# The row of 1/rms made by two transfers through HBM

## Chip, cores and metric

One core of one Trainium2 chip runs the whole program. The metric is the device time of the program in microseconds (us). TensorE (PE) multiplies matrices and reads its weights through a load path of its own (PEld), VectorE (DVE), ScalarE (ACT) and GpSimd (POOL) work element by element, SyncE (SP) issues transfers. Every engine runs its own list of instructions in order, and an instruction that waits holds up all that stand behind it on that engine.

## The reference

Two layers of a block over 512 tokens with 1024 channels. Each layer normalizes the tokens by their root mean square, projects them into five kinds of columns (pooled inputs, queries, keys, values, two gates), mixes, and closes with a gated feed-forward part:

```
def rmsnorm(x, g):
    xf = x.astype(jnp.float32)
    y = xf * lax.rsqrt(jnp.mean(xf * xf, axis=-1, keepdims=True) + NORM_EPS)
    return (y * g.astype(jnp.float32)).astype(x.dtype)

xn = rmsnorm(x, norm1_g[i])
proj = xn @ w_in[i]
u_pool, q, k, v, g_a, g_b = jnp.split(proj, splits, axis=-1)
...
merged = jax.nn.sigmoid(g_a) * pool_out + jax.nn.sigmoid(g_b) * attn_out
x = x + merged @ w_out[i]
```

The scale 1/rms is one number for each token.

## The kernel before

Every matrix product is made of three: operands are split into a rounded half and the rest (`whi`, `wlo` of the weights, `xh`, `xl` of the activations, `qh`, `ql` of queries and keys), and high by high, high by low and low by high are added up in PSUM. L289 to L291 and L308 to L310 are these three matmuls; a weight block of 512 KB is loaded into `raw` (L225, one of 7 buffers), cast by ACT into `whi`, and DVE makes `wlo` of it (both L213).

The activations go into the products without the 1/rms of their tokens; it is applied to what comes out. `token_stats` (L439, L440) sums squares on PE and lets POOL make `stats[:, 1, :]`, a tile in which partition p, column t holds 1/rms of token 128 t + p. Where a product has tokens on the partitions (queries, keys, values, the second gate), ACT and DVE scale by such a column. The pooled inputs and the first gate are made with tokens along the free axis (`windowed`, L714, and `merged`, L748); these need 1/rms as a row of 512 that stands on all 128 partitions. That row is `rms_rows[layer]`, the second half of a tile named `hg`, made once a layer by `spread_rms` (L500 to L506): four transposes on PE (L315) of the columns, each broadcast over 128, into a PSUM bank, and a copy by ACT (L506).

The order of the work is written with a counter of PE columns, `clock`: each matmul or transpose adds what it takes (a transpose 256). `later(delay, what)` asks for a piece of work when the counter has gone on by `delay`; before each triple of matmuls, `run_due` runs what is due. `spread_rms` is asked for 81600 columns behind a layer's start. Between the program's text and each engine's list stands the framework's scheduler, which settles where an instruction stands when the program is built; so a transfer can stand in SP's list well ahead of where the counter would put it.

SP's list holds the loads of weights and the turning of blocks of queries, keys, probabilities and outputs: DVE turns them in squares of 32, then a transfer takes them to HBM (`away`, L324) and four bring them back (`near`, L328). A load waits until its `raw` buffer is free, that is, until `wlo` of an earlier block is made. In layer 0 the first queries and keys are turned on PE (L315, `ident,qn`) and not through HBM.

The functions that the change touches, and what calls them:

Of the kernel before, what the change touches and what calls it, by code (L numbers as in the profile page):

```python
# [10 lines left out]
F32 = mybir.dt.float32  # L11
# [7 lines left out]
P = 128  # L19
# [3 lines left out]
NT = S // P  # L23
# [31 lines left out]

QK_AWAY, SCORE_AWAY, PROB_AWAY, AV_AWAY, MERGE_AWAY = 28000, 26000, 32000, 18000, 24000
NORMED, ROTATED, JOINED, GATED, SUMMED, GATE = 7200, 2400, 2400, 4800, 9600, 2400
HIDDEN_DELAYS = (26000, 28000), (8000, 14000)


# [64 lines left out]
def trunk_kernel(  # L125
# [10 lines left out]
    nc = tc.nc  # L136
# [3 lines left out]
    hbm = ctx.enter_context(tc.tile_pool(name="hbm", bufs=1, space=bass.MemoryType.DRAM))  # L140
# [29 lines left out]
    rotary, rms_rows = {}, {}  # L170
# [5 lines left out]
    def head_gains(layer):  # L176

        g = sb.tile([P, 2, S], F32, name="hg", tag="hg")
        rms_rows[layer] = g[:, 1, :]
        cs, sn = rotary[layer] = [g[:, 0, i * VD:(i + 1) * VD].rearrange("p (a t r) -> p a t r", a=2, t=NT) for i in range(2)]  # L180
        row = sb.tile([P, 2, ROT], F32, name="gr", tag="m12")
        for a in range(2):
            nc.sync.dma_start(row[:, a, :], spread(rows[layer][R_QG + QK * a:R_QG + QK * a + ROT]))
        for a in range(2):
            def times(to, table, gains):
                nc.gpsimd.tensor_tensor(to, table, gains.unsqueeze(1).broadcast_to(list(table.shape)), op=ALU.mult)
            times(cs[:, a], cos_t, row[:, a, :])
            for h in range(2):
                here, there = slice(h * HALF, (h + 1) * HALF), slice((1 - h) * HALF, (2 - h) * HALF)
                times(sn[:, a, :, here], sin_t[:, :, here], row[:, a, there])  # L190
        nc.gpsimd.tensor_tensor(gain_column(layer, 0), gain_column(layer, 0), gain_column(layer, 1), op=ALU.mult)
        nc.gpsimd.memset(gain_column(layer, 0)[:ROT], 1.0)
# [18 lines left out]
    def split(hi, lo, src):  # L211

        return nc.scalar.copy(hi, src), nc.vector.tensor_sub(lo, src, hi.bitcast(F32))  # L213
# [47 lines left out]
    def later(delay, what):  # L261
        heapq.heappush(waiting, (clock[0] + delay, count[0], what))
        count[0] += 1
# [50 lines left out]
    def transpose(dst, src):  # L314
        nc.tensor.transpose(dst, src, ident)  # L315
        clock[0] += 2 * P

    def turned(src, n, tag=None, bufs=1, near=None, wait=0):

        if near is None:  # L320
            near = sb.tile([P, n * P], F32, name="near", tag=tag, bufs=bufs)
        away = hbm.tile([P, n * P], F32, name="away", tag="away", bufs=8)
        nc.vector.transpose(near.rearrange("p (c k j) -> p k c j", c=4, k=n), src.rearrange("p (k c i) -> p k c i", k=n, c=4))
        nc.sync.dma_start(away, near)  # L324

        def back():
            for c in range(4):
                nc.sync.dma_start(  # L328
                    near[32 * c:32 * (c + 1), :].rearrange("i (q r) -> i q r", q=4),
                    away.rearrange("(q i) (c r) -> c i q r", q=4, c=4)[c])  # L330

        def back_behind():
            with tc.issue_after(transfers[-1].ins):
                back()

        if wait:
            later(wait, back_behind)
        else:
            back()
        return near.rearrange("p (q k j) -> p k q j", q=4, k=n)  # L340

    def squares_of(x):
        return x.rearrange("p k (q j) -> p k q j", q=4)
# [48 lines left out]
    def token(t):  # L392
        return slice(t * P, (t + 1) * P)
# [19 lines left out]
    stats = [None]  # L413
# [86 lines left out]

    def spread_rms(layer):

        row = tr_ps()
        for t in range(NT):
            transpose(row[:, token(t)], stats[0][:, 1, t:t + 1].broadcast_to([P, P]))
        nc.scalar.copy(rms_rows[layer], row)  # L506

    for layer in range(L):
        lam_init = 0.8 - 0.6 * math.exp(-0.3 * layer)
        if layer:  # L510
            head_gains(layer)
        later(81600, lambda layer=layer: spread_rms(layer))

        def x_tok(t):
            return [(xh[:, k, token(t)], xl[:, k, token(t)]) for k in range(KD)]
# [335 lines left out]
        class Hidden:  # L851
# [9 lines left out]
            def put(self, half, t, gate, up):  # L861
# [10 lines left out]
                if t:  # L872
                    back, done = HIDDEN_DELAYS[self.f0 >= GROUPS[-1] and self.f0 < ODD]
                    near = turned(h.rearrange("p i t c -> p (i t c)"), 4, ("up", "us")[half], 2, wait=back)
                    later(back + done, lambda: self.back(half, near))

            def back(self, half, near):

                with tc.issue_after(made[0].ins), tc.issue_after(made[1].ins):
                    split(*(squares_of(x[:, half].rearrange("p i c -> p (i c)").rearrange("p (k c) -> p k c", c=P))  # L880
                            for x in self.parts), near)
                ready.add((layer, self.f0, half))
# [222 lines left out]
```

## Time and profile before

| | |
|---|---|
| time, median of 3 runs | 1377.05 us (1376.94 to 1377.32) |
| profiled execution | 1376.3 us, its span 1374.5 us |
| granted clock of TensorE, mean | 1.000 |
| PE transposes of `stats` | 8, four at 53 us and four at 728 us |
| ACT copies of the row | 2, at 54.6 and 729.9 us |
| transfers | 224.07 MB, mean 163 GB/s |

The span runs from the first to the last instruction; the profiled execution's own time is 1.8 us more. "Chain" is the work that ended last, followed back from the end, at each step to what released it. A row of the timeline gives start, duration, engine, line, operation, what it writes and reads, and how many were merged; starts of matmuls are sure, their ends are modelled. A row of the list of transfers gives how many, the size of one in KB, and the median time in us from issue to landing.

### The profile page before, as it was taken

The page shows a single profiled execution, that of the slowest core. Times are in us where ns is not written, and L with a number is a line of the kernel's source. Part 1 is how long each engine was busy: PE and PEld are TensorE (multiplying, and loading weights), DVE is VectorE, ACT ScalarE, POOL GpSimd, SP SyncE. Part 2 cuts the span into 40 slices and gives each one's busy share as a digit, 9 for nine tenths or more (in the row PEclk, how much of TensorE's full clock was granted, in tenths as well). Part 3 has the DMA queues.
Part 4 walks back from the last instruction along what each step waited for, and adds up shares of the span by engine and source line. Part 5 has one row for each costly group of instructions (what it writes and reads, how often), then busy time and mean ns, then how long its engine had stood idle before and what let it go on. Part 6 is the DMA issues. An engine that isn't in the chain of part 4 may idle for free.

```text
span 1374.5 us, 18657 instructions
## 1 busy us (share of the span) xinstructions
PE 1369.2 (100%) x6238; PEld 1138.2 (83%) x6238; DVE 996.2 (72%) x1787; ACT 775.5 (56%) x1577; POOL 131.2 (10%) x155
## 2 busy tenths in 40 slices
PE   9999999999999999999999999999999999999999
PEld 7888888888888888888888888888888888888887
DVE  7668667687968768678666786765878687686782
ACT  7765554554757545554367755556557665555540
POOL 4010100000101101110010001010001111000100
PEclk9999999999999999999999999999999999999999
DMA  8244444444667968676435455444536788687831
GB/s 314 86 144 133 135 139 146 146 130 147 138 179 196 234 183 213 176 202 190 143 107 165 130 171 160 138 131 139 162 111 140 197 217 214 189 207 178 206 123 62
DMA packets 141072, 224.07 MB, mean 163 GB/s; under 512 B 41392, under 2 KB 88496, under 8 KB 140976
## 3 DMA queue, kind: packets, MB, share of 16 engines
q1 hardware_dynamic: 130464, 187.20, 42.7%
q0 software_dynamic: 9216, 33.56, 14.2%
q10 hardware_dynamic: 1296, 2.13, 0.6%
q8 instruction: 49, 0.80, 0.2%
q14 instruction: 47, 0.39, 0.1%
HBM read 193.59 MB, written 29.23 MB: 162 GB/s over the span
## 4 chain that ended last, share of the span: by engine, by line
PE 99%; DMA 0%; issue 0%; DVE 0%; ACT 0%; SPq 0%; ACTq 0%; DVEq 0%
PE mm L290 17%; PE mm L289 17%; PE mm L291 17%; PE mm L308 15%; PE mm L309 15%; PE mm L310 15%; PE mm L485 0%; PE mm L484 0%; PE mm L486 0%; PE mm L315 0%; PE mm L438 0%; DMA res<-in_x_t 0%; PE mm L493 0%; ACT ah L213 0%; DVE xh L473 0%
## 5 line engine op out<-in xcount | busy, mean ns | idle before, releaser
L213 DVE TENSOR_TENSOR wlo<-raw,whi 128x1024 fp32r<-128x1024 f32 (+1 forms) x220 | 266.8, 1217 | 75.7 <-ACT whi L213 74.9
L213 ACT CAST whi<-raw 128x1024 fp32r<-128x1024 f32 (+1 forms) x220 | 229.4, 1051 | 143.4 <-PE mm L291 75.0
L308 PE MATMUL mm<-whi,xh 128*128 128x512 f32 x480 | 188.8, 393 | 0.0
L310 PE MATMUL mm<-whi,xl 128*128 128x512 f32 x480 | 187.1, 390 | 0.0
L309 PE MATMUL mm<-wlo,xh 128*128 128x512 f32 x480 | 187.1, 390 | 0.0
L289 PE MATMUL mm<-whi,xh 128*128 128x512 f32 x384 | 149.6, 390 | 0.0
L291 PE MATMUL mm<-whi,xl 128*128 128x512 f32 x384 | 149.4, 389 | 0.0
L290 PE MATMUL mm<-wlo,xh 128*128 128x512 f32 x384 | 149.4, 389 | 0.0
L290 PE MATMUL mm<-fl,whi 128*128 128x512 f32 (+1 forms) x356 | 137.6, 387 | 0.0
L291 PE MATMUL mm<-fh,wlo 128*128 128x512 f32 (+1 forms) x356 | 137.6, 387 | 0.0
L289 PE MATMUL mm<-fh,whi 128*128 128x512 f32 (+1 forms) x356 | 137.6, 387 | 0.0
L767 DVE TENSOR_TENSOR res<-mm,res 128x512 f32<-128x512 f32 (+1 forms) x145 | 97.7, 678 | 44.0 <-PE mm L291 41.8
L353 POOL TENSOR_TENSOR r<-r,mhalf 128x4 f32<-128x4 f32 (+1 forms) x64 | 59.3, 929 | 512.0 <-DVE r L352 492.1
L239 POOL DMA_DIRECT2D wlo<-in_wts x64 | 56.1, 876 | 536.6 <-ACT wlo L238 363.0
L310 PEld LDWEIGHTS mm<-whi,xl 128*128 128x128 f32 x480 | 90.1, 188 | 19.2
L309 PEld LDWEIGHTS mm<-wlo,xh 128*128 128x128 f32 x480 | 90.3, 188 | 17.3
L308 PEld LDWEIGHTS mm<-whi,xh 128*128 128x128 f32 x480 | 90.2, 188 | 17.3
L308 PE MATMUL mm<-xh,whi 128*128 128x512 f32 x256 | 99.8, 390 | 0.0
L309 PE MATMUL mm<-xl,whi 128*128 128x512 f32 x256 | 99.8, 390 | 0.0
L310 PE MATMUL mm<-xh,wlo 128*128 128x512 f32 x256 | 99.6, 389 | 0.0
L291 PEld LDWEIGHTS mm<-whi,xl 128*128 128x128 f32 x384 | 72.1, 188 | 15.0
L290 PEld LDWEIGHTS mm<-wlo,xh 128*128 128x128 f32 x384 | 72.1, 188 | 15.0
(220 smaller groups left out, 2761.9 us busy)
## 6 DMA issues: line engine op xcount, KB each, us to landing
raw<-in_wts SPq DMA_DIRECT2D x243, 512.0 KB, 3.9
wlo<-in_wts POOLq DMA_DIRECT2D x64, 512.0 KB, 6.2
away<-near SPq DMA_DIRECT2D x73, 256.0 KB, 2.3
near<-away SPq DMA_DIRECT2D x292, 64.0 KB, 2.8
away<-near SPq DMA_DIRECT2D x29, 128.0 KB, 1.9
near<-away SPq DMA_DIRECT2D x116, 32.0 KB, 2.1
pwr<-in_pool_w ACTq DMA_DIRECT2D x8, 256.0 KB, 2.9
out<-res SPq DMA_DIRECT2D x7, 256.0 KB, 2.0
```

The source lines that it names most:

```text
L213: return nc.scalar.copy(hi, src), nc.vector.tensor_sub(lo, src, hi.bitcast(F32))
L239: nc.gpsimd.dma_start(lo.rearrange("p a b -> p (a b)"), wts[piece_no], accum_op=ALU.add)
L289: nc.tensor.matmul(acc, lhsT=ah, rhs=bh, start=start, stop=False, **check)
L290: nc.tensor.matmul(acc, lhsT=ah, rhs=bl, start=False, stop=False, **check)
L291: last = nc.tensor.matmul(acc, lhsT=al, rhs=bh, start=False, stop=stop, **check)
L308: nc.tensor.matmul(acc, lhsT=ah, rhs=bh, start=i == 0, stop=False)
L309: nc.tensor.matmul(acc, lhsT=ah, rhs=bl, start=False, stop=False)
L310: last = nc.tensor.matmul(acc, lhsT=al, rhs=bh, start=False, stop=i == n - 1)
L353: nc.gpsimd.tensor_tensor(r, r, mhalf[:, :width], op=ALU.pow)
L767: return nc.vector.tensor_add(res[d][:, cs], acc, res[d][:, cs])
```

## The change

`spread_rms` no longer uses PE, PSUM and ACT. A first transfer writes `stats[:, 1, :]` to a row of 512 numbers in HBM: each partition holds four numbers, and each of them goes to another place in the row, 128 numbers apart, so that all 512 are runs of four bytes. A second one, asked for 36000 columns later, reads that row (2 KB) into every partition of `hg`. `spread_rms` itself is asked for 72000 columns behind the layer's start, not 81600.

```diff
+ROW_BACK = 36000
...
     def spread_rms(layer):
 
-        row = tr_ps()
-        for t in range(NT):
-            transpose(row[:, token(t)], stats[0][:, 1, t:t + 1].broadcast_to([P, P]))
-        nc.scalar.copy(rms_rows[layer], row)
+        row = hbm.tile([NT, P], F32, name="row", tag="row", bufs=2)
+        nc.sync.dma_start(row.rearrange("t p -> p t"), stats[0][:, 1, :])
+
+        def back():
+            nc.sync.dma_start(rms_rows[layer], row.rearrange("t p -> (t p)").partition_broadcast(P))
+
+        later(ROW_BACK, back)
...
-        later(81600, lambda layer=layer: spread_rms(layer))
+        later(72000, lambda layer=layer: spread_rms(layer))
```

Line numbers behind the first edit go up by one, and behind `spread_rms` by four.

On SP, at the start of layer 0, before: the gains, four loads (values of the first head), the rows `lv`, and thirteen loads in one run, the first four of them for the next head's queries and keys.

```order
L183 DMA gr<-in_rows 128x32 x2
L225 DMA raw<-in_wts 128x1024 x4
L686 DMA lv<-in_rows 128x512 x2
L225 DMA raw<-in_wts 128x1024 x13
L324 DMA away<-near 128x512
```

And now, with what each one waits for (DMAHW: an earlier transfer of the same eighth; Pool, DVE: these engines):

```order
L690 DMA lv<-in_rows 128x512 [waits DMAHW3_49]
L505 DMA row<-stats 128x4x1 [waits DMAHW4_49,Pool_49]
L226 DMA raw<-in_wts 128x1024 [waits DMAHW5_49]
L226 DMA raw<-in_wts 128x1024 [waits DMAHW6_49]
L226 DMA raw<-in_wts 128x1024 [waits DMAHW7_49]
L226 DMA raw<-in_wts 128x1024 [waits DMAHW0_49,DVE_49]
L508 DMA hg<-row 128x512 [waits DMAHW4_49,DMAHW1_49]
L226 DMA raw<-in_wts 128x1024 [waits DMAHW2_49,DVE_49]
```

The first transfer stands right behind `lv` and waits for POOL, ahead of all thirteen loads; the second stands behind four of them and waits for the first to land.

On SP, at the start of layer 1, before: nine loads, then the first turned blocks of queries and keys.

```order
L324 DMA away<-near 128x512
L225 DMA raw<-in_wts 128x1024 x2
L328 DMA near<-away 32x4x128 x4
L225 DMA raw<-in_wts 128x1024 x9
L324 DMA away<-near 128x512 x2
L328 DMA near<-away 32x4x128 x8
```

And now:

```order
L226 DMA raw<-in_wts 128x1024 x9
L505 DMA row<-stats 128x4x1
L508 DMA hg<-row 128x512
L325 DMA away<-near 128x512 x2
L329 DMA near<-away 32x4x128 x8
```

Both transfers stand between the last load and the turning, the second right behind the first.

On PE, in layer 0, among the scores of the first head (`qh`, `ql`), before:

```order
L308 MATMUL mm<-qh 128x256
L309 MATMUL mm<-ql,qh 128x256
L310 MATMUL mm<-qh,ql 128x256
L315 MATMUL mm<-ident,stats 128x128 x4
L308 MATMUL mm<-qh 128x384
L309 MATMUL mm<-ql,qh 128x384
```

And now:

```order
L309 MATMUL mm<-qh 128x256
L310 MATMUL mm<-ql,qh 128x256
L311 MATMUL mm<-qh,ql 128x256
L309 MATMUL mm<-qh 128x384
L310 MATMUL mm<-ql,qh 128x384
```

The four transposes are gone, and the scores stand as they did.

## The prediction, made before the changed kernel was run

> **What bounds the kernel now.** I read the page's shares first, then the chain of work that ended last, then the list of what TensorE (PE) waited for.
>
> ```profile
> span 1374.5 us, 18657 instructions
> PE 1369.2 (100%) x6238; PEld 1138.2 (83%) x6238; DVE 996.2 (72%) x1787; ACT 775.5 (56%) x1577; POOL 131.2 (10%) x155
> PE 99%; DMA 0%; issue 0%; DVE 0%; ACT 0%; SPq 0%; ACTq 0%; DVEq 0%
> PE mm L405 <- DVE us L718: 1.2, 1, 1.2
> PE mm L493 <- DVE xh L473: 0.6, 1, 0.6
> ```
>
> The chain is PE at 99%, and the last two rows are the whole list of PE's waits: 1.8 us, both at the program's start, before either of the places that change. So after its first operands PE never stands still. What comes off PE's stream shortens the kernel by as much, as long as nothing new makes PE wait; what is added to another engine or to a queue costs nothing until it does.
>
> **What goes: two groups of four transposes on PE, and two copies on ACT.** The chain in order of time holds both groups of transposes, one in each layer:
>
> ```profile
> 53.26 0.44 PE mm L315 x4
> 727.76 0.44 PE mm L315 x4
> ```
>
> The timeline of PE lets me check that 0.44 us, since only the starts of matmuls are sure and a transpose's own row (0.60 us for four) overlaps its neighbours:
>
> ```profile
> 52.98 0.28 PE L310 MATMUL mm<-qh,ql 128*128 128x256 f32 x1
> 53.10 0.60 PE L315 MATMUL mm<-ident,stats 128*128 128x128 f32 x4
> 53.45 0.42 PE L308 MATMUL mm<-qh 128*128 128x384 f32 x1
> 53.71 0.34 PE L309 MATMUL mm<-ql,qh 128*128 128x384 f32 x1
> 53.89 0.34 PE L310 MATMUL mm<-qh,ql 128*128 128x384 f32 x1
> ```
>
> From the start of the last 256-wide matmul (52.98) to the second 384-wide one (53.71) are 0.73 us. Without transposes that is one 256-wide step, 0.12 (52.98 to 53.10), and one 384-wide step, 0.18 (53.71 to 53.89): 0.30. The difference is 0.43, and the chain says 0.44. I take 0.44 a layer, 2 x 0.44 = **0.88 us**. The matmuls behind are the same ones as before, so nothing else on PE gets shorter.
>
> The copies are
>
> ```profile
> L506 ACT COPY hg<-mm x2: 567/581/595, 54.6 to 729.9; 128x512 f32<-128x512 f32 x2
> L714 DVE TENSOR_TENSOR up<-mm,hg x16: 678/683/693, 116.2 to 1002.5; 128x512 f32<-128x512 f32 x16
> ```
>
> or 1.16 us of ACT, which is 56% busy and off the chain: worth 0. The second row tells when the row of 1/rms is first read, at 116.2 us. Layer 1 reads it first at its own windowed sums:
>
> ```profile
> L714 DVE TENSOR_TENSOR up<-mm,hg x4: 678/681/683, 796.5 to 889.3; 128x512 f32<-128x512 f32 x4
> ```
>
> **When the new row is there.** It can start once POOL has made 1/rms:
>
> ```profile
> 22.43 2.01 POOL L440 TENSOR_TENSOR stats<-stats,mhalf 128x4 f32<-128x4 f32 x1
> 702.02 1.04 POOL L440 TENSOR_TENSOR stats<-stats,mhalf 128x4 f32<-128x4 f32 x1 [54.49 <-DVE stats L439]
> ```
>
> that is, at 24.44 and 703.06 us. The built order puts the second transfer four loads behind the first in layer 0 and right behind it in layer 1, so the 36000 columns between them are not kept; both come some 85 us ahead of their readers (116.2 and 796.5). The pair can't be late.
>
> **What is added: two transfers a layer on SP's queue, and two waits there.** The trace has no transfer of four-byte runs. Nearest are
>
> ```profile
> pr<-away SPq DMA_DIRECT2D x24, 16.0 KB, 1.8
> away<-near SPq DMA_DIRECT2D x1, 64.0 KB, 1.5
> tab<-in_tables SPq DMA_DIRECT2D x1, 160.0 KB, 8.7
> lv<-in_rows SPq DMA_DIRECT2D x2, 256.0 KB, 7.9
> ```
>
> 16 KB in 128 runs of 128 bytes land in 1.8 us; the slowest, in full queues, take 8.7. If time went by the count of runs, 512 of them would be 4 x 1.8 = 7.2. I take 2 us for the first transfer (it is smallest and its queues are empty by then), with 1.5 and 8.7 as ends. The second is like lv in shape (one stretch of HBM spread over all partitions), and nobody waits for it.
>
> *Layer 0.* SP now stands at the first transfer until 24.44. Behind it are loads of weights, three of which went out from 16.00 on:
>
> ```profile
> 16.00 51.43 SPq L225 DMA_DIRECT2D raw<-in_wts  x13
> raw<-in_wts SPq DMA_DIRECT2D x3, 512.0 KB, 8.5
> raw<-in_wts SPq DMA_DIRECT2D x243, 512.0 KB, 3.9
> 30.66 2.01 ACT L213 CAST whi<-raw 128x1024 fp32r<-128x1024 f32 x2
> 47.83 1.04 ACT L213 CAST whi<-raw 128x1024 fp32r<-128x1024 f32 x1
> ```
>
> The second row is those three loads in their stretch: 8.5 us each, because the queues were still full of what came before. The third is all loads, 3.9. The first two of the three are cast by ACT at 30.66 and about 31.7, so they had lain there for some 6 us. Now they go out at about 24.9 and 25.3 (an issue holds SP for 0.3 to 0.4 us) into queues that have run empty, and land at 24.9 + 3.9 = 28.8 and about 30. Slack is left: 1.9 and 1.7 us. The third one and the next are cast at 47.83 or later.
>
> If they were late all the same, ACT would be late, and with it the fourth block of q and k, the next thing that PE takes from ACT:
>
> ```profile
> 38.58 0.28 DVE L390 TENSOR_TENSOR qn<-m 128x128 f32<-128x128 f32 x1
> 44.40 0.60 PE L315 MATMUL mm<-ident,qn 128*128 128x128 f32 x4
> ```
>
> It is done at 38.86 and used at 44.40: 5.5 us more. PE waits only if that load lands after 30.66 + 5.5 = 36.2, 11.3 us after its issue. Cost taken: 0.
>
> *Layer 1.* Here both transfers stand in a hole of SP's:
>
> ```profile
> 693.35 0.33 SPq L225 DMA_DIRECT2D raw<-in_wts  x1
> 707.55 1.84 SPq L324 DMA_DIRECT2D away<-near  x2
> 719.34 0.69 DVE L213 TENSOR_TENSOR ql<-near,qh 128x512 fp32r<-128x512 f32 x1 [1.80 <-ACT qh L213]
> 726.85 0.33 PE L308 MATMUL mm<-qh 128*128 128x256 f32 x1
> ```
>
> The first goes at 703.06, the second when it has landed, after L us, and SP is free at 703.06 + L + 0.4. The turning of q and k (away), queued behind, was issued at 707.55: it is not moved up to L = 4.0. What it brings is in ql at 719.34 + 0.69 = 720.03, and PE takes that second block at 726.85, 6.8 us later. So PE waits from L = 10.8 on; with 2 us SP has 2.1 to spare, and at 8.7 the queue slips 4.7, inside 6.8. Cost: 0 at both ends.
>
> *Order on PE.* The column counter loses 4 x 256 = 1024 a layer, so work asked for by that counter comes up to one triple of matmuls (0.7 us) later among its neighbours. The counter loses 0.46 us' worth where PE loses 0.44, so data is no less ready. Cost 0; a wait that opened here would take back up to the 0.88.
>
> **Sum.** 0.88 gained, 0 paid. The profiled execution took 1376.3 us (its span and 1.8 around it): 1376.3 - 0.9 = 1375.4. The median of the runs, 1377.05, is 0.75 above that one, so I give 1377.05 - 0.9 = **1376.1**. That is 0.065%, and a measurement of this kernel tells about 0.2% (2.75 us) from no change: the forecast counts as no change.
>
> **The rivals.** *Given back.* A shifted order or SP's slip opens a small wait on PE, of 0.5 to 1.5 us, and the time is 1376.6 to 1377.6. Against it: no wait on PE after the start, and slack of 5.5 and 6.8 us at the places touched. For it: so many instructions change places (PE, ACT, DVE, SP) that I can't check each.
>
> *The scattered write is slow: slower than before.* One mechanism, in layer 1: 512 separate words are written to HBM, SP stands at the second transfer, and the turning of q and k comes late. It decides from L = 10.8, costs 1 us a us from there, outweighs the gain at 11.7 and shows as slower at 10.8 + 0.9 + 2.75 = 14.4 us. With L = 16, 1377.05 - 0.9 + 5.2 = 1381.4. Against it: the largest landing in rows is 8.7, and 4 x 1.8 is 7.2. For it: no row has such short runs.
>
> The Trainium skill speaks against this edit in one place (DMA: Bandwidth & Descriptors, Rules for kernel authors): turning data is not to be done by "a plain DMA with a rearranged access pattern (19× difference)". An estimate by that page, 19 x 1.8 = 34 us for the first transfer, would put the wait of PE at 34 - 10.8 = 23 us and the time near 1399; no run here shows yet whether the factor holds for 2 KB.
>
> *It doesn't do what it says.* The 36000 columns between the transfers are in the code, not in the built queue. If the first is slow, four loads in layer 0 hide it and nothing does in layer 1. This changes no time at L under 10.8; it is the condition of the rival above, and not counted apart.
>
> *More than the transposes goes.* A gain of over 2.75 us needs three times what PE spends on them; no row has it.
>
> **Chances.** Forecast (1375.6 to 1376.6) 0.80; given back 0.12; slow write 0.05; more 0.03. Faster by over 0.2%: 0.02. Slower by over 0.2%: 0.05. Same: 0.93. The range goes from 0.75 under the forecast, for a chip or a run a little faster, over the given-back case: 1375.4 to 1377.6.
>
> **What would show it.** PE has 8 matmuls fewer, and no row of waits behind the start: right. In layer 0 the first transfer goes out at about 24.5, the loads behind it at 24.9, and ACT's casts stay near 30.7. In layer 1 it goes at about 703, the second at about 705, and the turning of q and k at 707 to 708. A landing of the first transfer of over 4 us, or a wait of PE on qh, ql or whi near 45 or 727 us, would show the step that failed. Unchanged times at 53 and 728, with PE's starts no closer, would make 0.44 wrong.

## The result, and the profile after

| | before | after |
|---|---|---|
| time, median | 1377.05 us (1376.68 to 1378.34) | 1388.46 us (1387.9 to 1392.79) |
| ratio | | 1.0089, 95% interval 1.0079 to 1.01 |
| profiled execution | 1376.3 us, span 1374.5 | 1388.39 us, span 1386.6 |

The change makes the kernel 11.4 us slower, where 0.9 us of gain was forecast. The longest of its five runs, 1392.79 us, had a mean granted clock of 0.995, the other four of 0.999. From the page of the changed kernel, the span, the busy times and the chain by engine:

```profile
span 1386.6 us, 18652 instructions
PE 1373.2 (99%) x6230; PEld 1138.2 (82%) x6230; DVE 995.5 (72%) x1787; ACT 773.4 (56%) x1575; POOL 129.3 (9%) x155
PE 85%; DVE 5%; DMA 3%; ACT 2%; POOL 2%; issue 1%; SPq 1%; DVEq 0%; ACTq 0%; POOLq 0%
```

The eight transposes are gone (6238 matmuls became 6230), but PE has only 85% of the chain where it had 99%: the rest goes over DVE, transfers, ACT and POOL. What PE waited for (total us, times, longest):

```profile
PE mm L309 <- ACT qh L214: 2.4, 1, 2.4
PE mm L309 <- ACT ah L214: 2.1, 1, 2.1
PE mm L406 <- DVE us L722: 1.2, 1, 1.2
PE mm L316 <- ACT lam L204: 1.1, 1, 1.1
PE mm L309 <- ACT pr L564: 1.1, 2, 0.8
PE mm L311 <- DVE al L214: 0.9, 2, 0.7
PE mm L494 <- DVE xh L474: 0.7, 1, 0.7
PE mm L310 <- DVE ql L214: 0.3, 1, 0.3
```

The third and the seventh row are those of before, at the program's start. All others are new; a ninth row, 0.2 us, is left out. The two transfers, by instruction (duration of the issue in ns, first and last start) and the time to landing of all four:

```profile
L505 SPq DMA_DIRECT2D row<-stats x2: 377/380/382, 25.1 to 706.9; - x2
L508 SPq DMA_DIRECT2D hg<-row x2: 327/327/327, 34.6 to 715.4; - x2
DMA to landing us min/median/max: 5.0/8.6/9.4
```

**Layer 0.** The list of transfers from 25 to 26 us, and from 26 to 35 (last column: median us to landing), and the chain in order of time (start, length):

```profile
raw<-in_wts SPq DMA_DIRECT2D x1, 512.0 KB, 12.9
row<-stats SPq DMA_DIRECT2D x1, 2.0 KB, 9.4
...
raw<-in_wts SPq DMA_DIRECT2D x4, 512.0 KB, 14.2
```

```profile
26.06 13.57 DMA raw<-in_wts
39.70 1.06 ACT whi L214
```

The write goes out at 25.08 and lands at 34.5. The first load behind it lands at 25.5 + 12.9 = 38.4, the next is on the chain until 39.6, and ACT casts it at 39.70, where before the casts began at 30.66 and 31.7. PE then waits 1.1 us ahead of the transposes (L316) of the fourth block of q and k, and again for probabilities.

**Layer 1.** SP's timeline (start, how long the group takes to issue):

```profile
706.93 0.38 SPq L505 DMA_DIRECT2D row<-stats  x1
715.37 0.33 SPq L508 DMA_DIRECT2D hg<-row  x1
715.79 0.86 SPq L325 DMA_DIRECT2D away<-near  x2
```

The list of transfers has a row of forty digits, each the busy share of the DMA engines in a fortieth of the stretch; from 706.5 to 715.3 us, 0.22 us a digit:

```profile
DMA  0000006400000000000000000000000000000000
```

The write's packets are over by 708.3 us, 1.3 us behind its issue; for the 7 us from there to its landing the DMA engines move nothing. SP stands 8.4 us until the write has landed, and the turning of q and k goes out at 715.79 where it went at 707.55 (PE itself is 3.8 us behind by then, so it slips by 4.4). The wait on PE does not come at 727, where that block is used, but 56 us later, at the second pair of heads. PE's timeline of the changed kernel there:

```profile
782.67 0.39 PE L309 MATMUL mm<-qh 128*128 128x256 f32 x1 [2.37 <-ACT qh L214]
783.39 0.39 PE L310 MATMUL mm<-ql,qh 128*128 128x256 f32 x1 [0.34 <-DVE ql L214]
```

and in the kernel before, DVE's row and PE's:

```profile
774.67 0.69 DVE L213 TENSOR_TENSOR ql<-near,qh 128x512 fp32r<-128x512 f32 x1 [0.91 <-ACT qh L213]
```

```profile
775.84 0.28 PE L309 MATMUL mm<-ql,qh 128*128 128x256 f32 x1
```

Before, ql was ready at 774.67 + 0.69 = 775.36 and used at 775.84: 0.5 us of slack, no wait in the list, and nothing that the list of waits could show. A second new wait, on `ah`, follows at 817 us; the run without a row will show it to be the order's, not the write's. Behind it the granted clock falls. Busy us by stretch; the last three columns are the clock, the transfers' share and GB/s:

```profile
820.00:823.50 3.50, 3.50 (x11) 2.77 (x10) 1.32 (x3) 1.79 (x4) 0.54 (x1) 0.56 0.19 43
```

From 820 to 823.5 the clock is 0.56: PE is busy all the time, but does 11 instructions where such a stretch holds 17 or more. 3.5 us at 0.56 are 1.5 us lost.

### The profile page after: what moved, and what is told of

The parts are those of the page before. It is cut to its first block, busy times and chain, and to the rows that moved or that the text cites. A ratio compares the mean times of both kernels' runs of the same rounds, so it can differ in the third digit from the quotient of the medians.

```text
span 1386.6 us, 18652 instructions
## 1 busy us (share of the span) xinstructions
PE 1373.2 (99%) x6230; PEld 1138.2 (82%) x6230; DVE 995.5 (72%) x1787; ACT 773.4 (56%) x1575; POOL 129.3 (9%) x155
## 4 chain that ended last, share of the span: by engine, by line
PE 85%; DVE 5%; DMA 3%; ACT 2%; POOL 2%; issue 1%; SPq 1%; DVEq 0%; ACTq 0%; POOLq 0%
PE mm L291 17%; PE mm L290 17%; PE mm L292 17%; PE mm L310 11%; PE mm L309 11%; PE mm L311 11%; DVE wlo L214 1%; DMA raw<-in_wts 1%; POOL r L354 1%; DMA away<-near 1%; DMA gr<-in_rows 1%; ACT whi L214 1%; SPq L329 1%; ACT qn L647 1%; DVE near L324 1%
```

## The experiments

Two things differ between the kernels beside the transposes: the transfers, and the order on PE, ACT and DVE that the counter settles. The first theory was that the write costs by its landing of 8 to 9 us; the rival, that the order costs. In the diffs a minus is the changed kernel, unless another is named.

### One layer at a time

```diff
+        if layer == 0:      # e2: if layer == 1
             row = hbm.tile([NT, P], F32, name="row", tag="row", bufs=2)
...
+        row = tr_ps()
+        for t in range(NT):
+            transpose(row[:, token(t)], stats[0][:, 1, t:t + 1].broadcast_to([P, P]))
+        nc.scalar.copy(rms_rows[layer], row)
```

> The two transfers in layer 0, the four transposes and the copy in layer 1 as before. Theory T (the scattered write lands after 8 to 9 us and what stands behind it on SP and in the transfer queues comes late): the write lands about 9.4 us after its issue, the loads behind it after 13 to 16 us, PE's starts are 3.4 to 3.9 us behind those of before from 140 us on, and the time is 1377.05 + 3.9 = 1381. If layer 1's waits near 780 and 815 us come from layer 0's delay or from the order, they are here too, and the time is near 1389. Rival O (the changed order of instructions makes the waits): about half of the loss, with waits near 780 and 815 us, since layer 0's transposes are gone alone.

> The two transfers in layer 1, transposes and copy in layer 0 as before. T: layer 0 as before, the write lands after 8.4 us at about 711 us, the turning of q and k goes out 4.4 us later than before, PE waits near 776 and 811 us, and the time is 1377.05 + 8 = 1385. O: the same waits, but with the transfers' landing playing no part.

Layer 0 alone: 1379.77 us, ratio 1.002 (1.001 to 1.003). Layer 1 alone: 1387.13, ratio 1.0074 (1.0059 to 1.0089). Theory T had 1381 and 1385; the waits near 780 and 815 us are there with layer 1's transfers alone and not with layer 0's. Both layers pay, layer 1 most. The layer that has the transfers has PE's order of the changed kernel too, the other that of before; so order and transfers are not apart yet. In layer 0 the write landed in 9.74 us; in layer 1 in 10.76, the point (10.8) from which the prediction let PE wait at 727 us; PE's first wait of that layer came ten us behind that block, at 737. The two losses add up to 12.9, more than the 11.4 of both.

### Without a row

```diff
-        row = hbm.tile([NT, P], F32, name="row", tag="row", bufs=2)
...
+        nc.scalar.copy(rms_rows[layer], res[0])
```

> The row of 1/rms is left out: ACT copies a tile of the same size in its place, so that the pooled inputs and the first gate are scaled by other numbers. PE's and SP's lists are those of the changed kernel without the four transfers. T: no wait on PE behind the start, 0.88 us less than before: 1376.2. O: waits near 58, 780 and 815 us as in the changed kernel, and 1385 to 1389.

1381.25 us, ratio 1.0035 (1.0022 to 1.0048), and TensorE's list is that of the changed kernel. No transfer and no transpose, and yet 4.2 us slower than before: neither forecast, 1376.2 or 1385 to 1389, was met. With the 0.88 of the transposes gone, **the order alone costs 5.1 us**, all of it in layer 1: in the profiled execution (1382.35 us) PE is level with before at the same column of work at 727 us, 0.4 us behind at 805, and 6.1 behind at 815. What lies between is one wait, and a slow clock behind it:

```profile
PE mm L309 <- ACT ah L214: 2.1, 1, 2.1
```

ACT's timeline shows how. Before, and then without a row:

```profile
803.29 0.51 ACT L213 CAST ah<-pr 128x384 fp32r<-128x384 f32 x1
...
809.75 0.62 ACT L752 ACTIVATE ta<-ta 128x512 f32<-128x512 f32 x1
```

```profile
809.07 0.63 ACT L750 ACTIVATE ta<-ta 128x512 f32<-128x512 f32 x1 [3.95 <-DVE ta L746]
809.61 0.49 ACT L214 CAST ah<-pr 128x384 fp32r<-128x384 f32 x1
```

In the other order the probabilities are turned 2.8 us later (at 798.57, not 795.74), and the cast `ah` now stands behind a gate's `ta` in ACT's list, which waits 3.95 us for DVE; before, that `ta` came 6 us behind `ah`. PE takes `ah` at 810.15, 2.14 us late. A granted clock of about a half follows here too:

```profile
813.00:816.50 3.50, 3.50 (x11) 2.73 (x10) 0.71 (x3) 1.56 (x4) 0.54 (x1) 0.50 0.17 38
```

With the stretches beside it (0.53 from 810 to 813 us, 0.92 from 816.5 to 820) the clock takes 3.4 us here, more than the wait. The execution took 1.1 us more than the median, so the clock's share in the 5.1 us is not sure.

### The write in runs of 16 bytes

```diff
-        row = hbm.tile([NT, P], F32, name="row", tag="row", bufs=2)
-        nc.sync.dma_start(row.rearrange("t p -> p t"), stats[0][:, 1, :])
+        row = hbm.tile([P, NT], F32, name="row", tag="row", bufs=2)
+        nc.sync.dma_start(row, stats[0][:, 1, :])
```

> The row is written as it lies, 128 runs of 16 bytes and not 512 of 4, and read back in that order; the tokens' order in the row is then wrong. All else stands where it stands in the changed kernel. T with the cost in the number of runs: the write lands four times as fast, after 2 to 3.5 us, the loads behind it in layer 0 land by 30 us, layer 1's turning isn't moved, and the time is 1376 to 1378. If the cost is a fixed one of writes under some size: the write lands after 8 us again and the time stays at 1388. If the landing is short and the time stays, the wait for POOL ahead of the loads in layer 0 is the cause there.

1380.85 us, ratio 1.0029 (1.0017 to 1.0041): that of the kernel without a row, within the runs. The forecast of 1376 to 1378 had left out what the order costs. The list of transfers around the write in layer 0:

```profile
raw<-in_wts SPq DMA_DIRECT2D x4, 512.0 KB, 6.8
row<-stats SPq DMA_DIRECT2D x1, 2.0 KB, 1.4
```

The same 2 KB, at the same places of the same queue, with the same wait of SP for the statistics: landed in 1.4 us, not 9.4, and the loads behind in 6.8, not 14.2. So neither the wait for POOL nor the second transfer is what costs, but the landing of the write.

### The other orders

Transfers added to the kernel before, whose transposes and copy stay (minus is before):

```diff
+        later(72000, lambda layer=layer: by_hbm(layer))
         later(81600, lambda layer=layer: spread_rms(layer))
```

> The kernel before with the two transfers of each layer added (the second right behind the first in the code, at 72000 columns); transposes and copy stay and write the row once more. PE's, ACT's and DVE's lists are those of before, SP's has the four transfers more. T1 (the slow write alone costs, whatever the order): layer 0 as in the run with layer 0 alone, 3.9 us, and layer 1 costs again, since the turning of q and k goes out 4 us late: 1377.05 + 4 to 8 = 1381 to 1385. T2 (the loss in layer 1 is the changed order's, and the write's delay is hidden in the order of before): about 1381, with no waits near 776 and 811 us beyond the 0.24 that is there.

The row left out as above, but the counter goes on by the transposes' columns:

```diff
+        clock[0] += 2 * P * NT
+        nc.scalar.copy(rms_rows[layer], res[0])
```

> As the run without a row, with the column counter put forward by the 1024 columns that the four transposes had added; ACT copies another tile in the row's place, so pooled inputs and first gate are scaled by other numbers. A third order: nearer to that of before on PE, not the same, since the built order also goes by the scheduler's own times. O (a wait at 775 and 808 us comes from the order that the missing 1024 columns make): these waits are gone or smaller, and the time is 1376.2 to 1378. If any order but that of before costs the same, 1381.

The changed kernel with the same columns added to the counter:

```diff
+        later(9600, lambda: clock.__setitem__(0, clock[0] + 2 * P * NT))
```

> The changed kernel with the column counter put forward by 1024 columns. Against the run before this one it has the same order and the transfers more: T expects 4 us more for layer 0's write, and in layer 1 what the late turning of q and k costs in this order: 1380 to 1386. If the write's price in layer 1 depends on the order, it differs here from the 3 to 5 us that it takes in the changed kernel's order.

| kernel | median us | ratio (95% interval) |
|---|---|---|
| before + transfers | 1386.24 | 1.0068 (1.0052 to 1.0085) |
| no row, counter kept | 1377.75 | 1.0005 (0.9996 to 1.0014) |
| changed, counter kept | 1387.06 | 1.0074 (1.0059 to 1.0089) |

The transfers cost 1386.24 - 1377.08 = 9.2 us in the order of before, 1387.06 - 1377.75 = 9.3 with the counter kept, and 1388.46 - 1381.25 = 7.2 in the order of the change. Both kernels with transfers came out above their forecasts (up to 1385 and up to 1386), the one without a row within its own. Why the write costs 2 us less in the order of the change was not tried; in the traces 1 us of it lies at `ah`, where the clock takes 3.4 us without a row and half of that in the changed kernel. (The 0.24 us of the first forecast: PE of before starts at 814.21, 0.47 behind the start ahead of it where 0.23 is usual; the list of waits has no row for it.) With the counter kept the order costs little: what is left of it takes the 0.88 back. At the same column of work, PE of the second kernel of the table is 0.47 us ahead of before at 770 us and 1.03 behind at 800: 1.5 lost at the second pair of heads, and 1377.08 - 0.88 + 1.5 = 1377.7.

### What makes the write slow

A chain of transfers behind the last output of the kernel before, each waiting for the one ahead; the first write is that of the change:

> The kernel before, and behind its last output a chain of small transfers between SBUF and HBM, each waiting for the one ahead: 512 runs of 4 bytes that lie side by side as in the change (twice), 128 runs of 16, 512 of 4 that are 8, 64 or 512 bytes apart, 128 of 4, 256 of 8. The span is longer by the chain and is not compared. If the landing goes by the number of runs: 8 us for all with 512, 4 for 256, 2 for both with 128. If it goes by neighbours in one stretch of memory that wait for each other: 8 us for those side by side, under 3 us for 64 and 512 bytes apart.

SP's timeline; from one start to the next is the landing of the first:

```profile
1373.14 0.43 SPq L1061 DMA_DIRECT2D rows<-res  x1
1382.39 0.34 SPq L1062 DMA_DIRECT2D ss<-rows  x1
1384.91 0.32 SPq L1064 DMA_DIRECT2D runs<-ss  x1
1386.31 0.32 SPq L1065 DMA_DIRECT2D ss<-runs  x1
1388.75 0.62 SPq L1067 DMA_DIRECT2D apart<-ss  x1
1392.56 0.58 SPq L1068 DMA_DIRECT2D ss<-apart  x1
1394.93 0.55 SPq L1070 DMA_DIRECT2D apart<-ss  x1
1397.34 0.54 SPq L1071 DMA_DIRECT2D ss<-apart  x1
...
1404.06 0.33 SPq L1076 DMA_DIRECT2D one<-ss  x1
1411.17 0.33 SPq L1077 DMA_DIRECT2D ss<-one  x1
```

512 words side by side: 9.25 us. 128 runs of 16 bytes: 1.4. 512 words 8 bytes apart: 3.8; 64 bytes apart: 2.4. Only 128 words side by side: 7.1. Behind these lines, 512 words 512 bytes apart took 2.1, 256 runs of 8 bytes 2.95, and the first write once more 8.4. So it is not the count of runs, which is 512 in three of the rows: single words that are **neighbours in HBM** are slow to land. One thing these writes do not separate: in the slow ones neighbouring words come from different partitions, in those with gaps mostly from the same one; whether that counts was not tried.

### Who is held

If the write held only its own queue, asking for it on ACT's would free SP's transfers.

```diff
-        nc.sync.dma_start(row.rearrange("t p -> p t"), stats[0][:, 1, :])
+        nc.scalar.dma_start(row.rearrange("t p -> p t"), stats[0][:, 1, :])
```

> The changed kernel with the first transfer asked for by ACT instead of SP; the second stays on SP and still stands right behind its five loads in layer 0 and, in layer 1, now behind two of the blocks (away) instead of ahead of them. So SP no longer waits for POOL's statistics in layer 0, and no load stands behind the slow write in its queue. Theory A (the slow write costs time because it holds back the transfers that are issued behind it on the same engine's queue, and SP itself through the read): in layer 0 five loads go near 16 us as before the change, but SP still stands at the read until the row has landed near 35, and eight loads wait behind it; some of the 3.2 us of layer 0 remains, the rest of layer 1 is mostly gone: 1382 to 1385. Theory B (the slow write loads the memory itself, whichever queue it comes by): the loads under way while it runs land 10 us late too, and the time stays within 1 us of 1388.5.

The write on SP again, not read back, over the kernel without a row:

```diff
+    def write():
+
+        row = hbm.tile([NT, P], F32, name="row", tag="row", bufs=2)
+        nc.sync.dma_start(row.rearrange("t p -> p t"), stats[0][:, 1, :])
...
+        later(72000, write)
         later(81600, lambda layer=layer: spread_rms(layer))
```

> The changed kernel's write on SP at its places, but nobody reads the row back: the gains get a copy of a part of res instead (as in e3_no_row), so the part left out is the use of 1/rms in them. TensorE's list is that of the changed kernel. SP has nothing to wait for behind the write. If what costs in layer 1 is SP standing at the read-back (8.4 us) with the blocks behind it, then away goes at 707.5 and lands some 2 us later, layer 1 costs only the order's part, and the time is e3's 1381.25 plus layer 0's 3.2, 1384.5. If the queue itself holds what is issued behind the write, away lands only when the row has, near 716, and the time is that of the changed kernel, 1388.5 within 1 us.

The write on ACT as above and the read held back, without and with the counter kept:

```diff
-ROW_BACK = 36000
+ROW_BACK = 90000
...
+            with tc.issue_after(transfers[-1].ins):
+                nc.sync.dma_start(rms_rows[layer], row.rearrange("t p -> (t p)").partition_broadcast(P))
...
+        later(9600, lambda: clock.__setitem__(0, clock[0] + 2 * P * NT))      # e12 alone
```

> The changed kernel with the first transfer asked for by ACT, and the read-back asked for 90000 columns behind it, tied to the end of a later block transfer, so that in layer 0 it stands behind eight more loads and in layer 1 behind two blocks. Nothing that others need stands behind the write or the waiting read. The counter is still 1024 columns a layer short, so TensorE's list is that of the changed kernel. If the 11.4 us are 5 of the order and 7 of the write's hold, the order's part is left: 1381.3 (1380.5 to 1382.5), as in e3_no_row. If the write costs something of itself that is not the hold, it stays above 1385.

> As e11_act_and_held, with the 1024 columns of the four transposes added to the counter again, so that TensorE's list is that of e6_no_row_counter_kept. Both suspected costs are out and the transposes are gone too: if the two account for the whole loss, the time is that of e6_no_row_counter_kept, 1377.7 (1377.0 to 1378.5), level with the kernel before. If something of the transfers costs beside the hold and the order, it is above 1380.

| kernel | median us | ratio (95% interval) |
|---|---|---|
| write on ACT | 1385.46 | 1.0068 (1.0053 to 1.0083) |
| write unread | 1387.42 | 1.0075 (1.0058 to 1.0092) |
| on ACT, read held back | 1385.02 | 1.0062 (1.0047 to 1.0077) |
| the same, counter kept | 1381.8 | 1.0039 (1.0024 to 1.0054) |

The write on ACT lies above theory A (up to 1385) and 3 us under theory B, so neither had it. The unread write costs nearly as much as the read one, 1387.42 us: near the 1388.5 of a queue that holds what stands behind, far from the 1384.5 of SP standing at the read; its two blocks, asked for at 713.55 and 715.06 us, landed within 1.1 us of the row, near 721. With the write on ACT, PE is level with before or ahead at 731 us (0.01 behind, 0.16 and 0.81 ahead in the three): layer 0 costs nothing any more. But layer 1 still does. Of the last two 1381.3 and 1377.7 had been expected, and about 4 us more were measured in each: the other case of both forecasts, in which the write costs something beside the hold of its queue. The lists of transfers of the third of them, from 706 to 709.5 us and from 28 to 30, say why:

```profile
DMA  0000000000187820000000000000004899999920
away<-near SPq DMA_DIRECT2D x2, 256.0 KB, 9.3
...
raw<-in_wts SPq DMA_DIRECT2D x1, 512.0 KB, 10.7
```

ACT asked for the write at 706.00; two blocks that SP asked for at 707.85 and 709.36 landed after 9.3 us (mean), where 2.0 is usual. In the row of digits (0.09 us each) the left group is the write's packets, the right one those of the first block: its bytes were moved by 709.4, and it landed at 717.6. So what is held is the landing, and not by the write's queue alone. In layer 0 the load in the last row was asked for at 28.59, **ahead** of the write on the other queue at 30.55, and landed 10.7 us later, where the load before it took 3.9. That full queues held it is unlikely: with a quick write (the next kernel below) the load at this place took 4.6. But in the kernel with the counter kept a load asked for at 27.91, as far ahead of the write at 29.88, landed in 4.5: not every transfer in flight is held. Two more runs asked whether such a write holds other queues, and a third for what could be won at best.

The kernel of the last row with the write in runs of 16 bytes, and DVE reading the row in that order:

```diff
-            nc.vector.tensor_mul(up[:, 16:], acc, rms_rows[layer])
+            by_token(up[:, 16:], acc, rms_rows[layer])
...
+    def by_token(to, acc, gains):
+        nc.vector.tensor_mul(to.rearrange("q (t p) -> q t p", t=NT), acc.rearrange("q (t p) -> q t p", t=NT), gains.rearrange("q (p t) -> q t p", t=NT))
```

> As e12_act_held_counter, but the write goes out as 128 runs of 16 bytes (each partition's four words side by side), and DVE's two multiplications read the row in that permuted order, so that each token gets its own 1/rms. TensorE's list is that of e12_act_held_counter. If the slow write holds the landings of every queue, and that is what e12 pays over e6_no_row_counter_kept, the write now lands in 1.4 us, the blocks behind it in layer 1 in 2 us, and the time is e6's 1377.7 (1377.0 to 1378.5) plus what DVE's strided read may cost. If the rest came of the move to ACT or of the read-back, it stays near 1381.8.

1378.88 us, ratio 1.0014 (1.0005 to 1.0024). Against 1.0039 with the slow write at the same place, 0.0025 or 3.4 us come back (the two intervals just touch), although DVE got slower. Its transfers from 706 to 709.5 us (the write, asked for at 705.88, is in the same list), and DVE's row:

```profile
away<-near SPq DMA_DIRECT2D x2, 256.0 KB, 2.0
row<-stats ACTq DMA_DIRECT2D x1, 2.0 KB, 1.4
```

```profile
L503 DVE TENSOR_TENSOR up<-mm,hg x16: 1045/1052/1083, 116.1 to 1004.9; 128x512 f32<-128x512 f32 x16
```

The blocks land in 2.0 us again. The strided read costs DVE 1.05 us where it took 0.68, 32 times, and PE has new waits that the kernel without a row and with the counter kept has not, 0.4 us in all on `ml` and 0.4 on `al`, both DVE's; they go some way to the 1.1 us over the kernel without a row and with the counter kept (1377.75), but nothing was run to show that they are all of it.

Hold by itself, behind the last output of the kernel before:

```diff
+    def beside(write, back):
+        x = block[0]
+        if write:
+            write(x[:, :NT])
+        nc.sync.dma_start(small("ss4", 4), x[:, :NT])
+        nc.sync.dma_start(sb.tile([P, S], F32, name="ta", tag="ta", bufs=2), x)
```

> The kernel before, and behind its last output a chain of probes; the time of the whole is not compared. Each link asks on SP for a copy of 2 KB and a copy of 256 KB between places in SBUF, the first two links of a round with nothing beside them or with a write of 128 runs of 16 bytes asked for on ACT at the same moment, the third with the write of 512 words of 4 bytes side by side on ACT; two rounds. If a write holds only its own queue, SP's copies land in 2 to 2.5 us in all links. If it holds the landings of every queue, they land in 2 to 2.5 us in the first and second link and in 8 to 9 us in the third.

The lists of transfers of three stretches: beside a write of 16-byte runs, beside the write of words, and beside the latter a second time.

```profile
ta<-up SPq DMA_DIRECT2D x1, 256.0 KB, 2.3
ss<-up SPq DMA_DIRECT2D x1, 2.0 KB, 1.7
runs<-up ACTq DMA_DIRECT2D x1, 2.0 KB, 1.4
...
ta<-up SPq DMA_DIRECT2D x1, 256.0 KB, 10.9
ss<-up SPq DMA_DIRECT2D x1, 2.0 KB, 1.6
words<-up ACTq DMA_DIRECT2D x1, 2.0 KB, 11.2
...
ta<-up SPq DMA_DIRECT2D x1, 256.0 KB, 8.6
words<-up ACTq DMA_DIRECT2D x1, 2.0 KB, 8.8
```

A block between two places in SBUF, asked for by SP some 0.4 us behind the write, lands when the write on ACT's queue has landed: 10.9 and 8.6 us, against 2.3. The copy of 2 KB, issued 0.05 and 0.14 us ahead of the write, gets away; my forecast had it held too. The Trainium skill says that transfers of all engines run on the same 16 DMA engines (DMA: Bandwidth & Descriptors, Issuing engines are not separate DMA queues). These rows fit that, and add that a slow landing on one queue delays the landing of what is asked for behind it on another.

What the saved transposes can give where the order stays near that of before (minus is before; the write is the one in 16-byte runs, the product as above):

```diff
-        for t in range(NT):
-            transpose(row[:, token(t)], stats[0][:, 1, t:t + 1].broadcast_to([P, P]))
-        nc.scalar.copy(rms_rows[layer], row)
+        transpose(bank[:, token(0)], stats[0][:, 1, 0:1].broadcast_to([P, P]))
+        clock[0] += 2 * P * (NT - 1)
+        nc.scalar.copy(small("sso"), bank[:, :1])
```

> The write in runs of 16 bytes on SP with the read-back 36000 columns behind it, and, to keep the order of the kernel before, one of the four transposes stays (its result is not used), the other three columns' worth is added to the counter, and ACT copies one column where it copied the row. TensorE's list is that of before less three transposes a layer up to the third group of layer 1, with single products moved by a place or two behind. What the removed transposes can give is 2 x 3 x 0.11 = 0.66 us. If that is kept: 1376.0 to 1376.4. If the waits of layer 1's second head, where before has 0.24 us of waiting already, take it back: 1376.6 to 1378.

1379.17 us, ratio 1.0015 (1.0006 to 1.0025): slower than both cases of the forecast, which left out DVE's strided read. PE waits at the second pair of heads (0.6 on `qh`, 0.3 on `ql`), as without a row and with the counter kept, and on `ml` and `al` (0.5 and 0.4), as with the strided read above. No kernel that was run beats the one before.

## Why the prediction was wrong

The sum of the loss, from medians: -0.88 for the transposes, +5.1 for the order, +7.2 for the write in that order, together 11.4. Of the write's 7.2, layer 0 has 3.2 by the run with that layer alone, which leaves about 4 to layer 1. The prediction had both the write and the order at 0.

- **0.88 us for the transposes: right.** At the same column of work, PE of the kernel without a row is 0.65 us behind before at 52.5 us and 0.21 at 56, 0.03 behind at 727 and 0.41 ahead at 729: 0.44 at each group. In the changed kernel it is 3.84 and 3.40 behind at the last two.
- **"I take 2 us for the first transfer": wrong.** It took 9.4 and 8.4. The bound by counts of runs, 7.2, and the upper end, 8.7, were near; I chose the value by size, and the row of 1.8 us that I scaled by runs (`pr<-away`) reads HBM, where the new transfer writes it. That 7.2 lies near is luck: 128 words alone took 7.1. The "19×" of the Trainium skill (DMA: Bandwidth & Descriptors, Rules for kernel authors) compares with the hardware's own transposing transfer, which no run here has; as a warning it had the right sign. 8.4 to 9.4 over the 1.8 us of the 16 KB transfer is about 5, and the runs show that the neighbours decide.
- **Layer 0, "into queues that have run empty", landing at 28.8 and 30: wrong.** Behind the slow write a load lands when the write has landed and its own 3.9 us are over: 34.5 + 3.9 = 38.4. The point given for PE's wait, a load behind 36.2, held: PE waited. By the run with this layer alone it loses 2.77 + 0.44 = 3.2 us. The condition was worked out; that the loads behind the write would wait for its landing was left out.
- **Layer 1, "Cost: 0 at both ends": wrong, and not by its landing.** L was 8.4, inside 10.8, and at 727 us PE did not wait, as said. But 6.8 us was the slack of one consumer. Everything behind in the queue slipped too, the work of ACT, DVE and POOL on it with it, and the second pair of heads had 0.5 us in the order of before and none in the new one, where PE waits 0.3 us on `ql` even without a row. Between 731 and 776 us PE loses 4.3 us against before in the changed kernel and 0.8 without a row: the write's part is 3.4, and 2.4 of it is lost at the second pair, 56 us after the place that I had looked at. The wait on `ah` is not the slip's: it is 2.1 us without a row too.
- **"Order on PE ... Cost 0; a wait that opened here would take back up to the 0.88": wrong, 5.1 us.** I held the cost to the size of the removed work. What changed was whether the cast `ah` or a gate's `ta` stood first in ACT's list; `ta` waits 3.95 us for DVE, `ah` with it, PE 2.1 us for `ah`, and then PE's clock falls.
- **Rivals.** The slow write was the one on the other side, but with the wrong place and the wrong threshold: it needed no L over 10.8. "It doesn't do what it says" was called the condition of that rival and no more; the unread write (ratio 1.0075 against 1.0089) shows that even a read kept far behind would have saved little.

What the half clock costs (1.7 us in the changed kernel's trace, 3.4 without a row) is read from the traces only: no run kept the waits and took the drop of the clock away, and why it follows some waits and not others stays open. Which part of the hold lies with the DMA engines and which with the memory was not tried either.

## What to carry to other kernels

A transfer's price has two parts, its own landing and what it does to the landings of transfers beside it, on whichever queue; where it writes single words side by side, write runs of 16 bytes and leave the turning to the reader, if the reader can afford it. Slack worked out at the first consumer holds for that consumer only: before a queue is let slip, look for the smallest slack on the way to the end, also where the list of waits is empty. An edit that shifts a counter is a change of order, and its cost goes by the waits in the lists that change places and by what the clock does behind them, not by the work that went.

## What the hardware did that I had not expected

- 2 KB written to HBM as 512 words side by side landed in 8.4 to 11.2 us, though its packets were over 1.3 us behind the issue; 128 words side by side landed in 7.1, 2 KB as 512 words 64 bytes apart in 2.4, as 128 runs of 16 bytes in 1.4.
- While such a write was under way, transfers asked for on another engine's queue landed late as well: 8.6 and 10.9 us for a block of 256 KB within SBUF that takes 2.3; a load asked for 2 us ahead of it took 10.7 in one run and 4.5 in another.
- After waits of PE of 2.1 us and some tenths right behind, the granted clock was about a half for some us (0.56 from 820 to 823.5 us in the changed kernel, 0.50 from 813 to 816.5 without a row). After the wait of 2.4 us at 782 in the changed kernel it stayed at 1.00. In the traces of the kernels above PE has 14 single waits of 1.9 to 2.4 us behind the start: with 9 of them the clock fell to 0.50, from 0.2 us ahead of the wait's end to 2.3 us behind it, for 3.4 or 6.8 us; with 5 it did not. Beside shorter waits, 1.4 us at most, it did not fall before the program's end.
- DVE's product of 128x512 took 1.05 us with one operand read in steps of 16 bytes, 0.68 with it read in order.
